# Which queue stores the kept input differences of a two-layer encoder, and when the first input of the down product is split

## The chip, the cores and the metric

The kernel runs on one core of one Trainium2 chip. The core has a matrix engine (TensorE, PE in the profile), a vector engine (VectorE, DVE), an activation engine (ScalarE, ACT), a general engine (GpSimd, POOL) and SyncE (SP), which here only issues DMAs. Each engine works through its own queue in order; ACT, POOL and SP can put DMAs into theirs. The metric is the device time of one execution in microseconds, lower is better.

## The reference

Two encoder layers over 256 tokens of width 2048. Each has an attention sub-layer and an MLP with squared ReLU of width 8192; the change touches the MLP.

```python
for i in range(DEPTH):                      # DEPTH = 2
    h = rms_norm(x, norm_attn[i])
    ...                                     # token mixer and memory attention, one input projection
    x = x + heads @ w_out[i]
    h = rms_norm(x, norm_mlp[i])
    x = x + jnp.square(jax.nn.relu(h @ w_up[i])) @ w_down[i]
```

## The kernel before

**Numbers.** Every float32 operand of a product is split into a high part and a low part (`split`, L441 to L443: ACT casts to the high part, DVE subtracts it for the low part), and a product is three matmuls: high by high, high by low, low by high (`three`, L533 to L536). Weights come from memory as pieces of 128 x 1024 and are split on the chip (`fetch`, L369), two pieces ahead of the one in use (`AHEAD`).

**The MLP** (`mlp`, L997) has two products. `up` makes the 8192 hidden columns in eight steps q of 1024 columns; each step has eight pairs j of inputs. `down` runs over 32 pairs j of hidden inputs, twice, once for each half of the output columns (`half_`).

**Seven instead of eight.** For some pairs (`UP_FAST`, `FAST`, `LATE`) the block product of a pair takes seven block multiplications in place of eight (`seven`, L551). It needs sums of weight blocks (`sum_pair`, L347: four quads, a high and a low part of each of two sums) and differences of input blocks (`differences`, L541: three DVE operations, then a split). For `down`, some of the weight sums are made ahead of time in device memory by POOL's queue (`make_sums`, L285): a copy of one block (L291), and one step later, when the copy has landed, a DMA that adds another block to it (L295). These run during the projections, `out` and `up`; in layer 1 they come closer together during `up` than in layer 0 (`SUM_GAP`: 7 pieces apart, 11 in layer 0).

**Kept differences.** The input differences of `down` are computed while `up` runs, soon after a hidden block exists, and are stored in device memory; both halves of `down` read them back (`load_kept`, L1119 to L1122, POOL's queue, two pairs ahead). There are 17 in each layer (`FAST`), 512 KB each. `keep` (L1008) takes a quad of the tag `h2`, computes the differences into it, and issues the store from POOL's queue (L1013). `to_hidden` (L1023), which transposes a step's result, applies ReLU and square, and may store the hidden block too (L1037, POOL), hands `keep` to the scheduler of small work as one stage.

**Small work.** A `Task` is a list of stages. `tick` (L209) is called twice after every pair; it counts a clock, and runs the stages that are due. A `Light` stage runs at its tick whatever else does; its gap is the number of ticks until the next stage of its task is due.

**Buffers.** `quad` (L91) gives tiles of 4 KB a partition; the tag `h2` has six. During `up` they hold the four parts of a pair's weight sums, the differences of one input pair of `up` (`diffs[2]`, until pair 2 of q = 7), and a kept difference on its way out. During `down` they hold the split inputs (`h2_of`, L1083) and the kept differences read back. The Tile framework gives a tile its place and inserts the waits: whoever writes a place first waits until its last reader, a DMA too, is done. It also settles the order of each engine's queue, near the program's order.

**The boundary of up and down.** After the last pair of q = 7, `own_add` (L1018, four DVE operations, L1021) adds the shared sums to the step's result, and the transposes of `to_hidden` (L1031) read that. Then `down` begins: `load_kept(1)`, the split of input 0 (`ats = deque([h2_of(0)])`, L1125), and from then on the split of input j + 1 while pair j is worked on (L1131). The same lines begin the second half.

Of the kernel before, what the change touches and what calls it, by code (L numbers as in the profile page):

```python
# [15 lines left out]
F32R = mybir.dt.float32r  # L16
# [6 lines left out]
P = 128  # L23
# [30 lines left out]
LOOK = 3  # L54
KEEP_AFTER = (2, 6, 10, 14)
KEEP_LAST = (10, 18, 26, 34)
SUM_AT = {0: 44, 1: 2}
SUM_GAP = ({"in": 4, "mem": 4, "out": 4, "up": 11}, {"in": 4, "mem": 12, "out": 12, "up": 7})
LAM_INIT = 0.8 - 0.6 * math.exp(-0.3 * 0)
# [11 lines left out]
def trunk(ctx: ExitStack, tc: tile.TileContext, xin, xtok, memin, memtok, posrel, gcol, rows,  # L71
# [12 lines left out]
    def nm(s):  # L84
        uid[0] += 1
        return f"{s}{uid[0]}"
# [4 lines left out]
    def quad(tag, shape=(P, 2, 2, 256), dt=F32R):  # L91
        return xp.tile(list(shape), dt, tag=tag, name=nm(tag), bufs={"x2": 8, "h2": 6, "blk": 10}[tag])
# [83 lines left out]
    def Light(f, gap):  # L176
        return Stage(f, gap, gap, True)
# [819 lines left out]
    def mlp(layer, X2, last):  # L997
# [7 lines left out]
        def hidden(j):  # L1005
            return hT[j // 2].rearrange("p k s -> p (k s)")[:, (j % 2) * 512:(j % 2) * 512 + 512]

        def keep(j):  # L1008

            t2 = quad("h2", (P, 2, 512))  # L1010
            differences(t2, hidden(j))
            kept[j] = dp.tile([P, 2, 512], F32R, name=nm("kept"))
            nc.gpsimd.dma_start(kept[j], t2)  # L1013

        name = f"up{layer}"
        diffs = {}
# [6 lines left out]
        def to_hidden(q, n, u, i, tag):  # L1023
            c = 2 * q + n
            if i == 0:
                hT.append(wide[:, 5] if c == 15 else blk([P, 4, S], F32))
            pt = bank(tag)
            for oo in range(2):
                for t in range(2):
                    o = 2 * i + oo  # L1030
                    nc.tensor.transpose(out=pt[:, oo * S + t * P:oo * S + (t + 1) * P], in_=u[n][t][:, o * P:(o + 1) * P], identity=ident)  # L1031
            j = 2 * c + i
            nc.scalar.activation(hidden(j), pt, AF.Relu)
            nc.scalar.activation(hidden(j), hidden(j), AF.Square)
            if c in AWAY:
                hidden_in[j] = dp.tile([P, 512], F32, name=nm("hid"))
                nc.gpsimd.dma_start(hidden_in[j], hidden(j))  # L1037
            if any(j in fast_pairs(f"down{layer}", h) for h in range(2)):
                Task([Light(lambda: keep(j), 0)], wait=KEEP_AFTER[2 * n + i] if q < 7 else KEEP_LAST[2 * n + i])

        for q in range(8):
            tag, other = ("mm", "aux") if q % 2 == 0 else ("aux", "mm")
            own = [[bank(tag) for _ in range(2)] for _ in range(2)]
            fast = UP_FAST[q]
            for j in range(8):
                if j == fast[0]:
                    side = [bank(other) for _ in range(4)]
                if q == 0 and j in DIFF_UP:
                    i = DIFF_UP[j]
                    diffs[i] = quad("h2" if i == 2 else "blk", (P, 2, 512))  # L1050
                    pair_differences(X2.pairs[i], diffs[i])
                two = [piece(name, q, 2 * j + i) for i in range(2)]
                pair = X2.pairs[j]

                def at(kk, t, part):
                    return pair[:, kk, part, t * P:(t + 1) * P]

                if j in fast:
                    seven(own, side, j == fast[0], j == fast[-1], two, sums.pop((name, q, j)), at, diffs[j])
                elif j < 7:  # L1060
                    for kk in range(2):
                        for t in range(2):
                            for n in range(2):
                                one_of_eight(own, n, t, 2 * j + kk, KT - 1, two, at)
                else:
                    for n in range(2):
                        for t in range(2):
                            for kk in range(2):
                                one_of_eight(own, n, t, 2 * j + kk, KT - 1, two, at)
                if j == fast[-1]:  # L1070
                    u = side_sums(side)
                for _ in range(2):
                    tick(2)
            own_add(own, u)
            if q == 0:
                mlp_stats()
            Task([lambda q=q, u=u, n=n, i=i, tag=tag: to_hidden(q, n, u, i, tag) for n in range(2) for i in range(2)], wait=1, gap=0)
        slots.append(blk([P, 4, S], F32))
        N2 = Halves()
        while making:  # L1080
            making.popleft()[1]()

        def h2_of(j):  # L1083
            t2 = quad("h2", (P, 2, 512))
            split(t2[:, 0, :], t2[:, 1, :], hids.pop(j) if j in hidden_in else hidden(j))
            return lambda kk, t, part: t2[:, part, kk * S + t * P:kk * S + (t + 1) * P]

        for half_ in range(2):
            tag = "mm" if half_ == 0 else "aux"
# [32 lines left out]
                    nc.gpsimd.dma_start(diff_in[j], kept[j])  # L1122

            load_kept(1)
            ats = deque([h2_of(0)])  # L1125
            for j in range(32):
                if j == fast[0]:
                    side = [bank("aux" if half_ == 0 else "mm") for _ in range(4)]
                two = [piece(f"down{layer}", half_, 2 * j)]
                if j < 31:  # L1130
                    ats.append(h2_of(j + 1))  # L1131
                load_kept(j + 2)
                two.append(piece(f"down{layer}", half_, 2 * j + 1))
                at = ats.popleft()
# [184 lines left out]
```

## Time and profile before

| | us |
|---|---|
| median of 3 runs | 2078.95 |
| lowest and highest | 2076.1, 2083.54 |
| the profiled execution | 2079.43 |
| its span | 2077.6 |

The times are those of whole executions. The profile is of one execution; its span leaves out 1.8 us around it. An engine's busy time is the time in which it executes instructions; a matrix multiplication's own length overlaps with the next, so two of them start closer together than one is long. Issues of DMAs stand in the queue rows (ACTq, SPq, POOLq, or POOL with a DMA's name) and the time from issue to landing in rows of their own. In the rows of a timeline the brackets hold the idle time of the engine ahead of the instruction and what ended it. The chain of waits goes back from the last instruction, at each step to what released it.

The DMAs that the change touches or that stand in their way, by the profile's list of issues:

| DMA | queue | count | KB | median us to landing |
|---|---|---|---|---|
| kept differences out | POOL | 34 | 512 | 6.8 |
| kept differences in | POOL | 64 | 512 | 5.9 |
| made sums, copy and add | POOL | 124 | 512 | 6.5 |
| hidden blocks out | POOL | 36 | 256 | 4.7 |
| weights of up, plain pairs | SP | 164 | 512 | 5.8 |
| first gains, the only one of ACT | ACT | 1 | 8 | 2.5 |

### The profile page before, as it was taken

Reading aid. Unit: us, or ns where it says so; the run is one execution under the profiler, and the core shown is the slowest. Engines: PE = TensorE matmul, PEld = TensorE weight load, DVE = VectorE, ACT = ScalarE, POOL = GpSimd, SP = SyncE. Lnnn points to the kernel's source line nnn. Section 1 sums busy time; section 2 is a strip of 40 time slices with the busy share of each in tenths; the row PEclk is TensorE's granted clock in tenths of the full one; section 3 lists DMA queues with packets and bytes.
Section 4 is the critical chain, followed back from the end, with each engine's and each line's share of the span. In section 5 each row is a group of like instructions: output and inputs, shape, how many; then the busy total and the mean of one; then the engine's idle time right before and its main releaser. Section 6 shows DMA issues by size and latency. Waiting matters only on the chain.

```text
span 2077.6 us, 28751 instructions
## 1 busy us (share of the span) xinstructions
PE 2068.8 (100%) x9996; PEld 1718.0 (83%) x9996; DVE 1790.4 (86%) x2583; ACT 1280.2 (62%) x1906; POOL 193.2 (9%) x301
## 2 busy tenths in 40 slices
PE   9999999999999999999999999999999999999999
PEld 7888888888888888888888888888888888888887
DVE  7677778898999999998886678889999889999998
ACT  7466665556655676666655556566556567766764
POOL 1201111100010010000001110000101111000000
PEclk9999999999999999999999999999999999999999
DMA  9678988877887789988978987568889998998994
GB/s 312 244 241 276 272 291 232 269 232 218 272 291 259 237 293 329 357 289 282 326 265 273 267 252 228 187 223 244 262 273 293 303 286 309 328 363 309 306 356 168
DMA packets 170641, 572.28 MB, mean 275 GB/s; under 512 B 19744, under 2 KB 20768, under 8 KB 169248
## 3 DMA queue, kind: packets, MB, share of 16 engines
q1 hardware_dynamic: 132976, 440.41, 59.8%
q0 software_dynamic: 37376, 130.04, 23.4%
q8 instruction: 78, 1.28, 0.2%
q14 instruction: 67, 0.55, 0.1%
q10 hardware_dynamic: 144, 0.01, 0.0%
HBM read 537.74 MB, written 97.65 MB: 306 GB/s over the span
## 4 chain that ended last, share of the span: by engine, by line
PE 92%; DMA 2%; DVE 2%; issue 2%; ACT 1%; SPq 0%; POOL 0%; ACTq 0%; DVEq 0%; POOLq 0%
PE mm L535 11%; PE mm L534 11%; PE mm L536 11%; PE aux L535 11%; PE aux L536 11%; PE aux L534 11%; PE mm L495 7%; PE mm L496 7%; PE mm L497 7%; DMA kept<-h 1%; DVE lo L443 1%; PE aux L638 1%; PE mm L1031 1%; PE aux L615 1%; PE aux L657 1%
## 5 line engine op out<-in xcount | busy, mean ns | idle before, releaser
L443 DVE TENSOR_TENSOR lo<-raw,hi 128x1024 fp32r<-128x1024 f32 (+1 forms) x512 | 607.6, 1207 | 168.3 <-ACT hi L442 166.7
L442 ACT CAST hi<-raw 128x1024 fp32r<-128x1024 f32 (+1 forms) x512 | 515.3, 1036 | 377.7 <-PE mm L497 113.9
L495 PE MATMUL mm<-hi,x 128*128 128x512 f32 x640 | 256.7, 403 | 0.7 <-ACT hi L442 0.7
L496 PE MATMUL mm<-lo,x 128*128 128x512 f32 x640 | 250.8, 392 | 0.0
L497 PE MATMUL mm<-hi,x 128*128 128x512 f32 x640 | 250.3, 391 | 0.0
L442 ACT CAST h<-big 128x1024 fp32r<-128x1024 f32 (+1 forms) x100 | 101.1, 1020 | 145.0 <-DVE big L283 90.2
L535 PE MATMUL aux<-lo,h 128*128 128x512 f32 x440 | 171.5, 390 | 0.2 <-DVE lo L443 0.2
L534 PE MATMUL aux<-hi,h 128*128 128x512 f32 x440 | 171.6, 390 | 0.0
L536 PE MATMUL aux<-hi,h 128*128 128x512 f32 x440 | 171.4, 389 | 0.0
L534 PE MATMUL mm<-hi,h 128*128 128x512 f32 (+1 forms) x438 | 170.1, 389 | 0.9 <-ACT h L442 0.9
L535 PE MATMUL mm<-lo,h 128*128 128x512 f32 (+1 forms) x438 | 169.8, 388 | 0.0
L536 PE MATMUL mm<-hi,h 128*128 128x512 f32 (+1 forms) x438 | 169.5, 388 | 0.0
L534 PE MATMUL mm<-hi,x 128*128 128x512 f32 x414 | 161.9, 391 | 0.0
L535 PE MATMUL mm<-lo,x 128*128 128x512 f32 x414 | 161.5, 390 | 0.2 <-DVE lo L443 0.2
L536 PE MATMUL mm<-hi,x 128*128 128x512 f32 x414 | 161.3, 390 | 0.0
L442 ACT CAST hi<-big 128x1024 fp32r<-128x1024 f32 (+1 forms) x146 | 128.9, 911 | 47.8 <-issue 24.5
L535 PE MATMUL aux<-lo,x 128*128 128x512 f32 x398 | 155.3, 390 | 0.5 <-DVE lo L443 0.5
L534 PE MATMUL aux<-hi,x 128*128 128x512 f32 x398 | 155.7, 391 | 0.0
L536 PE MATMUL aux<-hi,x 128*128 128x512 f32 x398 | 155.1, 390 | 0.0
L443 DVE TENSOR_TENSOR lo<-big,hi 128x1024 fp32r<-128x1024 f32 (+1 forms) x146 | 149.1, 1044 | 4.3 <-ACT hi L442 4.3
L497 PEld LDWEIGHTS mm<-hi,x 128*128 128x128 f32 x640 | 120.2, 188 | 26.0
L495 PEld LDWEIGHTS mm<-hi,x 128*128 128x128 f32 x640 | 120.5, 189 | 24.6 <-ACT hi L442 1.1
(310 smaller groups left out, 4268.6 us busy)
## 6 DMA issues: line engine op xcount, KB each, us to landing
raw<-in_w_up SPq DMA_DIRECT2D x164, 512.0 KB, 5.8
raw<-in_w_down SPq DMA_DIRECT2D x128, 512.0 KB, 5.6
madesum<-in_w_down POOLq DMA_DIRECT2D x124, 512.0 KB, 6.5
big<-in_w_up SPq DMA_DIRECT2D x92, 512.0 KB, 4.6
raw<-in_w_a SPq DMA_DIRECT2D x72, 512.0 KB, 4.7
h<-kept POOLq DMA_DIRECT2D x64, 512.0 KB, 5.9
big<-in_w_down SPq DMA_DIRECT2D x54, 512.0 KB, 5.2
big<-madesum SPq DMA_DIRECT2D x53, 512.0 KB, 5.3
```

Source lines behind the costliest of these rows:

```text
L442: nc.scalar.copy(hi, src)
L443: return nc.vector.tensor_tensor(lo, src, as32(hi), op=ALU.subtract)
L495: nc.tensor.matmul(ps[t], lhsT=xh, rhs=hi[:, ws], start=(k == 0), stop=False)
L496: nc.tensor.matmul(ps[t], lhsT=xh, rhs=lo[:, ws], start=False, stop=False)
L497: nc.tensor.matmul(ps[t], lhsT=xl, rhs=hi[:, ws], start=False, stop=(k == KT - 1))
L534: nc.tensor.matmul(acc_, lhsT=x(0), rhs=w2[0][:, ws], start=first_, stop=False)
L535: nc.tensor.matmul(acc_, lhsT=x(0), rhs=w2[1][:, ws], start=False, stop=False)
L536: nc.tensor.matmul(acc_, lhsT=x(1), rhs=w2[0][:, ws], start=False, stop=last_)
L615: nc.tensor.transpose(out=pt[:, h * P:(h + 1) * P], in_=qn[t][:, h * P:(h + 1) * P], identity=ident)
L638: nc.tensor.transpose(out=pt[:, kt * S + qt * P:kt * S + (qt + 1) * P], in_=p_of(qt)[:, kt * P:(kt + 1) * P], identity=ident)
L657: nc.tensor.matmul(ps[c][:, qt * S:(qt + 1) * S], lhsT=qT[a][r, hl, qs], rhs=kT[b][r, hl, :], start=(a + b == 0), stop=(a == 1))
L1031: nc.tensor.transpose(out=pt[:, oo * S + t * P:oo * S + (t + 1) * P], in_=u[n][t][:, o * P:(o + 1) * P], identity=ident)
```

## The change

Two edits, both in the MLP of both layers.

1. `keep` becomes a task of two light stages. `make` takes the quad and computes the differences when `keep` ran before. `store` follows two ticks later (`KEEP_GAP`) and issues the DMA from ACT's queue, source and destination named as plain float32.
2. The split of input 0 of `down` is made ahead of pair 7 of q = 7 in `up`, for the first half, and during pair 31 of the first half, for the second.

```diff
+KEEP_GAP = 2
...
-        def keep(j):
+        def keep(j, wait):
+
+            def make():
+                box.append(quad("h2", (P, 2, 512)))
+                differences(box[0], hidden(j))
+
+            def store():
+                kept[j] = dp.tile([P, 2, 512], F32R, name=nm("kept"))
+                nc.scalar.dma_start(as32(kept[j]), as32(box.pop()))
+
+            box = []
+            Task([Light(make, KEEP_GAP), Light(store, 0)], wait=wait)
 
+        def h2_of(j):
             t2 = quad("h2", (P, 2, 512))
-            differences(t2, hidden(j))
-            kept[j] = dp.tile([P, 2, 512], F32R, name=nm("kept"))
-            nc.gpsimd.dma_start(kept[j], t2)
+            split(t2[:, 0, :], t2[:, 1, :], hids.pop(j) if j in hidden_in else hidden(j))
+            return lambda kk, t, part: t2[:, part, kk * S + t * P:kk * S + (t + 1) * P]
...
-                Task([Light(lambda: keep(j), 0)], wait=KEEP_AFTER[2 * n + i] if q < 7 else KEEP_LAST[2 * n + i])
+                keep(j, KEEP_AFTER[2 * n + i] if q < 7 else KEEP_LAST[2 * n + i])
...
+                if q == j == 7:
+                    ats = deque([h2_of(0)])
                 two = [piece(name, q, 2 * j + i) for i in range(2)]
...
-        def h2_of(j):
-            t2 = quad("h2", (P, 2, 512))
-            split(t2[:, 0, :], t2[:, 1, :], hids.pop(j) if j in hidden_in else hidden(j))
-            return lambda kk, t, part: t2[:, part, kk * S + t * P:kk * S + (t + 1) * P]
-
...
             load_kept(1)
-            ats = deque([h2_of(0)])
             for j in range(32):
...
-                if j < 31:
-                    ats.append(h2_of(j + 1))
+                if j < 31 or half_ == 0:
+                    ats.append(h2_of((j + 1) % 32))
                 load_kept(j + 2)
```

## The prediction, made before the change was run

> **What bounds the kernel now.** I read the page's busy times first, then the time from one group of transposes to the next in both layers, then the chain of waits where that time is longer.
>
> ```profile
> span 2077.6 us, 28751 instructions
> PE 2068.8 (100%) x9996; PEld 1718.0 (83%) x9996; DVE 1790.4 (86%) x2583; ACT 1280.2 (62%) x1906; POOL 193.2 (9%) x301
> ```
>
> TensorE (PE) is busy for all but 9 us. Nothing that shortens another engine's work can gain more than the stalls that PE has left, so the first question is how many there are and who causes them. The up product repeats one period of work per step of q, with 16 transposes (L1031) in each. The chain of waits gives their instants, and the table of windows the two layers' six periods:
>
> ```profile
> 465.11 1.75 PE mm L1031 x16
> ...
> 724.58 1.75 PE mm L1031 x16
> ...
> 1487.42 1.75 PE aux L1031 x16
> ...
> 1575.80 1.75 PE aux L1031 x16
> ...
> 1619.04 1.75 PE mm L1031 x16
> ...
> 1708.56 1.75 PE mm L1031 x16
> ...
> 465.11:724.58 259.47, 259.47 (x1196) 216.38 (x1195) 239.71 (x288) 157.44 (x201) 22.57 (x36) 1.00 0.79 256
> ...
> 1444.18:1708.56 264.38, 261.86 (x1196) 215.83 (x1195) 237.09 (x286) 156.28 (x199) 35.52 (x52) 1.00 0.88 281
> ```
>
> The columns are length, busy time with instruction count of PE, weight loads, DVE, ACT and POOL, granted clock, DMA share, GB/s. Both windows hold 1196 matmuls. Layer 0 does them in 259.47 us, or 43.245 a period, with PE busy throughout; layer 1 takes 264.38. So layer 1 loses **4.91 us** here, at the same granted clock of 1.00. Two of its periods (1487.42 to 1575.80) take 88.38 instead of 86.49, a loss of 1.89; two more (1619.04 to 1708.56) take 89.52, a loss of 3.03. The chain of waits in the first stretch:
>
> ```profile
> 1547.01 1.08 POOL madesum L295
> ...
> 1548.91 11.84 DMA kept<-h
> 1560.85 1.06 ACT h L442
> 1561.93 1.24 DVE h L443
> ...
> 1563.21 0.50 PE mm L535
> ```
>
> This is read downwards. GpSimd issues the accumulating DMA of a made sum (L295), then the store of kept differences (L1013). The store lands 11.84 us later, and only then does ScalarE's cast into a quad begin, then VectorE's low part, then PE. Kept quads and the sums of the up product share six h2 quads: one for the first differences, four for a pair's sums, one for a kept input. A quad is free only when its store has landed. The timelines of ACT, DVE, POOL and PE show the three stalls:
>
> ```profile
> 1546.67 0.61 ACT L442 CAST h<-t2k 128x512 fp32r<-128x512 f32 x1
> 1547.47 2.00 ACT L442 CAST hi<-raw 128x1024 fp32r<-128x1024 f32 x2 [0.20 <-ACT h L442]
> ...
> 1560.85 1.05 ACT L442 CAST h<-big 128x1024 fp32r<-128x1024 f32 x1 [5.92 <-DMA kept<-h]
> ...
> 1640.07 0.62 ACT L442 CAST h<-t2k 128x512 fp32r<-128x512 f32 x1 [2.07 <-DMA kept<-h]
> ...
> 1680.26 2.00 ACT L442 CAST hi<-raw 128x1024 fp32r<-128x1024 f32 x2 [0.20 <-ACT h L442]
> ...
> 1693.04 1.05 ACT L442 CAST h<-big 128x1024 fp32r<-128x1024 f32 x1 [5.32 <-DMA kept<-h]
> ...
> 1547.94 0.68 DVE L443 TENSOR_TENSOR h<-t2k,h 128x512 fp32r<-128x512 f32 x1
> ...
> 1680.72 0.68 DVE L443 TENSOR_TENSOR h<-t2k,h 128x512 fp32r<-128x512 f32 x1
> ...
> 1631.88 0.56 POOL L1013 DMA_DIRECT2D kept<-h  x1
> ...
> 1642.96 0.50 PE L535 MATMUL aux<-lo,x 128*128 128x512 f32 x1 [0.53 <-DVE lo L443]
> ...
> 1695.41 0.50 PE L535 MATMUL aux<-h,blk 128*128 128x512 f32 x1 [0.71 <-DVE h L443]
> ...
> 1698.28 0.50 PE L535 MATMUL mm<-lo,x 128*128 128x512 f32 x1 [0.16 <-DVE lo L443]
> ```
>
> All three waits of ACT end with a store's landing. PE's idle times divide the 3.03 us of the later stretch as 0.53 to 0.87: 1.1 us for the second stall, 1.9 for the third. With 1.9 for the first, that is the whole 4.91.
>
> The other stall is where up ends and down begins, again in PE's and ACT's timelines:
>
> ```profile
> 762.23 1.93 PE L1031 MATMUL aux<-ident,t2k 128*128 128x128 f32 x16
> 764.83 0.50 PE L534 MATMUL mm<-hi,h 128*128 128x512 f32 x1 [0.67 <-ACT h L442]
> ...
> 763.64 0.61 ACT L442 CAST h<-t2k 128x512 fp32r<-128x512 f32 x1
> 764.17 1.13 ACT L442 CAST h<-blk 128x512 fp32r<-128x512 f32 x2
> ...
> 1746.35 1.14 PE L1031 MATMUL aux<-ident,t2k 128*128 128x128 f32 x9
> 1747.79 0.98 PE L1031 MATMUL aux<-ident,t2k 128*128 128x128 f32 x7 [0.29 <-DVE t2k L1021]
> 1748.95 0.50 PE L534 MATMUL mm<-hi,h 128*128 128x512 f32 x1 [0.19 <-ACT h L442]
> ...
> 956.50 0.50 PE L535 MATMUL aux<-lo,h 128*128 128x512 f32 x1 [0.18 <-DVE lo L443]
> ```
>
> Sixteen transposes at their pace of 1.75 us end at 763.98 in layer 0 and would end at 1748.10 in layer 1; the first matmul of down starts 0.85 us after that in each. In layer 0 the cast of down's first input (h<-blk) comes last. In layer 1 own_add on DVE (L1021) holds the transposes, and the cast holds the rest. The last row is PE's wait near the middle of layer 0's down, the one other place that the first input's move could touch.
>
> **The change, part by part.**
>
> *The stores.* 34 stores leave POOL and go to ACT's queue, each issued two ticks (one pair of inputs) after its differences. The rows on which their landing rests, from the kept tile in layer 1's window and in layer 0's, and from the issues of 1545 to 1562:
>
> ```profile
> DMA to landing us min/median/max: 6.2/9.0/11.8
> ...
> DMA to landing us min/median/max: 5.1/6.0/8.0
> ...
> raw<-in_w_up SPq DMA_DIRECT2D x2, 512.0 KB, 9.7
> ```
>
> No store on ACT's queue stands in this trace, so I bound its landing: 6.0 us from below (the store's median in layer 0, with few made sums on POOL) and 9.7 from above (weights of the same size from SP's queue, in the very stretch of the first stall). The issue moves too. In the first stall the low part is done at 1547.94 + 0.68 = 1548.6 and ACT has two casts behind the make, to 1549.5; the store goes out there instead of at 1548.91. It lands at 1555.5 to 1559.2. The landing now is 1560.85 and has to come 1.9 earlier, by 1558.95: 1.65 to 1.9 recovered. In the third, ACT's two casts end at 1682.3, so it lands at 1688.3 to 1692.0, against 1693.0 less 1.9: 1.0 to 1.9 recovered. In the second, issue stays about 1631.9 and the landing is 1637.9 to 1641.6, against 1640.0: all 1.1 recovered, or 1.1 more lost. Together 1.5 to 4.9. I take **4.0**, nearer the lower landing, because the store that was late had an accumulating DMA ahead of it in its own queue and will not have that on ACT's.
>
> The Trainium skill's "DMA: Bandwidth & Descriptors", section "Issuing engines are not separate DMA queues", speaks against this: all engines' DMAs run on the same 16 DMA engines and another issuer saves only issue time. By that rule alone the sum would lose its 4.0, since POOL issued the first late store 0.3 us after its data was ready. The same page, section "SWDGE vs HWDGE vs iDMA", says that the two kinds of queue feed different internal queues between which an engine turns in rotation; by that the 4.0 stands. No run here has yet shown a store on ACT's queue.
>
> *What the stores cost ACT.* The one DMA that ACT issues today, and what waiting does to an issuing queue:
>
> ```profile
> 0.74 0.41 ACTq L129 DMA_DIRECT2D gc<-in_gcol  x1
> ...
> SPq L387 <- DVE lo L443: 804.1, 403, 12.6
> ```
>
> 34 issues at 0.41 are 14 us of ACT, 17 a layer. In the up windows ACT is busy 157 of 259 us and its idle time is spent waiting for PE and DVE, which covers 13 x 0.41 = 5.3 us a window. The second row is the danger: a queue whose DMA waits for DVE stands still with all that is behind it, here the casts of the next weight pieces, for which DVE's low parts and then PE wait. The delay from the make's cast to the end of its low part is 1548.6 - 1546.67 = 1.95 us, and the two casts between make and store take 2.0, so the wait is mostly over when the store's turn comes. The bounds: nothing, or a standstill long enough to reach PE. The second stall measures that: 2.07 us of ACT's waiting cost 1.1 of PE, so about 1.0 us is free. I take 0. A later release of the quad can also delay the next make's cast by up to a pair's time; the same spare applies.
>
> *POOL* loses 34 issues of 0.56 us and has its made sums and reads alone. It bounds nothing, so I give that nothing.
>
> *The first input of down, a pair sooner.* Its cast (0.61) and low part (about 0.65) move ahead of pair 7 of q = 7. Nothing is added but the earlier use of an h2 quad, which is there, since pair 6's sums are read by then. In layer 0 PE can go on at once: up to 0.85 gained. If the transposes still run first, the 0.65 us on DVE ahead of own_add gives some 0.25 back: 0.6. I take 0.7. In layer 1 own_add is what the transposes wait for. If the first matmuls of down go ahead of the transposes, 0.85 is gained; if not, own_add ends 0.65 later and 0.25 is lost. I take 0.5. At the middle of down (half 0 to half 1) I give nothing: PE's idle time there is 0.18, and it ends with the low part of a weight piece, not of the input.
>
> *Sum:* 4.0 + 0.7 + 0.5 = 5.2 off the profiled execution's 2079.43, so 2074.2. That execution stands 0.5 above the median of the three runs, 2078.95; I forecast **2074.0**, between the two bases.
>
> **The rivals.**
>
> *All of it goes:* 4.9 + 0.85 + 0.85 = 6.6 off, and a few tenths more if other short waits fall with them: 2072.3. For it speaks that layer 0, with the same up product, has no stall at all; against it that DMA is at 0.88 in layer 1's window and 0.79 in layer 0's.
>
> *The landing is set by the traffic.* With the 9.7 us of SP's own loads in that stretch as the rule and the store issued up to a pair later, no net time is won in up: only the 1.2 at the boundaries stays, 2078.2. For it: the loads on SP's queue were as slow as the stores. The Trainium skill's section on issuing engines, named above, would have it so. Against it: those two loads shared SP's queue with others, while the store has ACT's to itself.
>
> *Slower: ACT's queue stands still at the stores.* Where DVE lags by more than about 1.0 us behind the store's place on ACT, or the next kept cast waits for a store issued a pair later, the casts of weights come late. The point from which it decides is that 1.0 us. Priced at what layer 1 loses today, layer 0's six periods lose 4.9 and layer 1's a second 4.9, less 1.2 at the boundaries: +8.6, 2088.0. Against it: the 1.95 us lag above, and ACT's being idle for 39% of the window.
>
> **How the numbers follow.** Forecast 0.50 (own range 2072 to 2077), all of it 0.20, traffic 0.20, slower 0.10. The range 2071 to 2081 leaves out the slower case, most of which lies above, and the far end of the full gain. 0.3%, which is 6.2 us, is about what a measurement of this kernel can tell from no change. Faster by more: 0.15 from the full gain, 0.05 from the forecast's better end, 0.20. Slower by more: 0.09, the last case less a part that costs less. The rest, 0.71, is within.
>
> **What would show it.** Right: layer 1's six up periods take 259.5 to 261 us; stores land in 6 to 8 us beside an accumulating DMA; ACT no longer waits 5 us for a kept landing; the transposes of the last q stand behind down's first matmuls, or without idle time ahead of them. Wrong: layer 0's 259.47 grows; DMA issues on ACT wait for DVE by more than 1 us; stores land in 9 us or more with the same stalls; the idle time before down's first matmul stays.

## The result, and the profile after

| | before | after |
|---|---|---|
| median of 9 runs, us | 2078.95 | 2072.9 |
| lowest and highest, us | 2076.1, 2083.54 | 2071.96, 2073.38 |
| the profiled execution, us | 2079.43 | 2072.64 |
| its span, us | 2077.6 | 2070.9 |

The ratio of the times is 0.9967, with a 95% interval of 0.9958 to 0.9977. That is 0.33% faster, or 6.05 us between the medians. The interval has the line of 0.3% inside it, so a change of more than 0.3% and one of less can barely be told apart here.

The profile after, first its page: the busy times, and the shares of the chain of waits by engine.

```profile
PE 2065.5 (100%) x9996; PEld 1718.5 (83%) x9996; DVE 1784.3 (86%) x2583; ACT 1278.6 (62%) x1906; POOL 173.7 (8%) x267
PE 99%; DMA 0%; DVE 0%; issue 0%; ACT 0%; SPq 0%; ACTq 0%; DVEq 0%
```

The same line of the chain before:

```profile
PE 92%; DMA 2%; DVE 2%; issue 2%; ACT 1%; SPq 0%; POOL 0%; ACTq 0%; DVEq 0%; POOLq 0%
```

The matmuls are the same 9996. What went is the 7% of the chain that passed through DMAs, casts, subtractions and issues. That is a share of the chain and not time won: PE was busy beside most of it. The windows show where time was won. First after, the six periods of up in layer 0 and in layer 1 (columns as in the prediction), then the 100 us that begin with the transposes of q = 6, for each layer:

```profile
464.68:724.16 259.48, 259.48 (x1197) 216.32 (x1195) 236.09 (x287) 156.36 (x200) 15.40 (x23) 1.00 0.78 256
1443.11:1702.59 259.48, 259.48 (x1196) 216.32 (x1195) 236.29 (x287) 156.63 (x200) 27.98 (x39) 1.00 0.89 286
...
724.16:824.16 100.00, 100.00 (x460) 83.33 (x458) 94.07 (x116) 71.43 (x95) 7.49 (x14) 1.00 0.88 308
...
1702.59:1802.59 100.00, 100.00 (x459) 83.33 (x458) 94.80 (x117) 72.22 (x96) 7.55 (x14) 1.00 0.92 317
```

The same 100 us before:

```profile
724.58:824.58 100.00, 99.33 (x455) 82.57 (x453) 94.05 (x116) 70.64 (x94) 9.64 (x18) 1.00 0.87 302
...
1708.56:1808.56 100.00, 99.52 (x455) 82.24 (x453) 94.51 (x118) 71.74 (x95) 9.68 (x18) 1.00 0.92 315
```

The six up periods of layer 1 fell from 264.38 to 259.48, the time of layer 0, at a DMA share that is no lower (0.89). All 4.90 us are back. In the 100 us around the end of up, PE starts 5 matmuls more in layer 0 and 4 more in layer 1. At 0.22 to 0.23 us from one start to the next (761.58 to 761.80 below) these 9 are about **2.0 us**, good to one matmul in each layer. Together that is 6.9; the spans differ by 6.7. The account isn't exact to a few tenths: the transposes that begin layer 0's window come 0.43 earlier (464.68 against 465.11), though neither edit touches what is ahead of them.

**The stores.** ACT's timeline where the first stall was, after:

```profile
1545.54 0.62 ACT L443 CAST h<-t2k 128x512 fp32r<-128x512 f32 x1
1546.41 2.00 ACT L443 CAST hi<-raw 128x1024 fp32r<-128x1024 f32 x2 [0.25 <-ACT h L443]
1547.53 0.33 ACTq L1017 DMA_DIRECT2D kept<-h  x1
```

Two things are to be seen. The store (L1017) goes out between the two casts of one group, not behind them. And it comes 17.93 us into its period (which begins at 1529.60), against 18.24 before (1548.91, in the period that began 43.25 after 1487.42). The list of DMA issues of that instant, after and then before, gives KB and the time to landing:

```profile
kept<-h ACTq DMA_DIRECT2D x1, 512.0 KB, 8.3
```

```profile
kept<-h POOLq DMA_DIRECT2D x1, 512.0 KB, 11.8
```

So here 3.5 of the 3.8 us by which the landing is earlier come from a shorter flight, and 0.3 from an earlier issue. The second stall went in another way. DVE's timeline before, with the low part that the store waits for, and DVE's and ACT's after:

```profile
1630.90 0.68 DVE L443 TENSOR_TENSOR h<-t2k,h 128x512 fp32r<-128x512 f32 x1
```

```profile
1625.43 0.68 DVE L444 TENSOR_TENSOR h<-t2k,h 128x512 fp32r<-128x512 f32 x1
...
1626.15 0.33 ACTq L1017 DMA_DIRECT2D kept<-h  x1
```

Before, the low part ends at 1631.58 and the store goes out at 1631.88, 12.84 us into its period; after, the low part ends at 1626.11 and the store goes out 0.04 us later, 10.05 into its period. So POOL's order didn't hold the store. Of the 2.8 us, 2.5 are that the differences themselves are made earlier, in another order of ACT's and DVE's work, and 0.3 is the issue. Two other runs with the store on ACT's queue, stores only and one stage, have the same 10.05; the runs with POOL's or SP's have 11.8 to 12.8. The flight is no shorter (8.8 after, 8.1 before). In the third stall the flight falls from 11.2 to 9.3 us, and the issue comes 0.3 earlier in its period. All 13 stores of layer 1's window (1443 to 1703) together, by the kept tile, after:

```profile
  DVE h L444: 1.9, 1
  ACT h L443: 0.4, 1
...
DMA to landing us min/median/max: 5.0/8.4/9.3
```

The first two rows are who waited for a store (us in all, times). Before, ACT waited 14.0 us in four times, and landings were 6.2/9.0/11.8. DVE's 1.9 now costs PE nothing, by the windows.

**The end of up**, PE's timeline in layer 0, and then in layer 1:

```profile
761.58 0.39 PE L537 MATMUL aux<-hi,x 128*128 128x512 f32 x1
761.80 0.39 PE L535 MATMUL mm<-hi,h 128*128 128x512 f32 x1
...
767.25 1.91 PE L1043 MATMUL aux<-ident,t2k 128*128 128x128 f32 x16
...
1740.00 0.39 PE L537 MATMUL aux<-hi,x 128*128 128x512 f32 x1
1740.23 0.39 PE L535 MATMUL mm<-hi,h 128*128 128x512 f32 x1
```

The last matmul of up (aux) is followed by the first of down (mm) at the usual distance, in both layers. The transposes (L1043) stand 5.45 us later, behind down's first pair, and nothing waits for own_add. Near the middle of layer 0's down, in PE's timeline after:

```profile
954.33 0.50 PE L536 MATMUL aux<-lo,h 128*128 128x512 f32 x1 [0.23 <-DVE lo L444]
955.46 0.50 PE L536 MATMUL aux<-lo,h 128*128 128x512 f32 x1 [0.17 <-DVE lo L444]
```

Two waits, 0.40 us, where before there was one of 0.18. That the sooner split causes the second isn't shown: with it and the stores on SP's queue there is one, of 0.17.

### The profile page after: what moved, and what is told of

It is laid out like the page before. It is cut to its first block, busy times and chain, and to the rows that moved or that the text cites. A ratio compares the mean times of both kernels' runs of the same rounds, so it can differ in the third digit from the quotient of the medians.

```text
span 2070.9 us, 28741 instructions
## 1 busy us (share of the span) xinstructions
PE 2065.5 (100%) x9996; PEld 1718.5 (83%) x9996; DVE 1784.3 (86%) x2583; ACT 1278.6 (62%) x1906; POOL 173.7 (8%) x267
## 4 chain that ended last, share of the span: by engine, by line
PE 99%; DMA 0%; DVE 0%; issue 0%; ACT 0%; SPq 0%; ACTq 0%; DVEq 0%
PE mm L537 12%; PE mm L536 12%; PE mm L535 12%; PE aux L536 12%; PE aux L537 12%; PE aux L535 12%; PE mm L496 7%; PE mm L497 7%; PE mm L498 7%; PE aux L639 1%; PE aux L1043 1%; PE mm L1043 1%; PE aux L616 1%; PE aux L658 1%; PE aux L696 1%; PE aux L845 0%
## 5 line engine op out<-in xcount | busy, mean ns | idle before, releaser
L498 PEld LDWEIGHTS mm<-hi,x 128*128 128x128 f32 x640 | 120.3, 188 | 26.1
L444 DVE TENSOR_TENSOR h<-big,h 128x1024 fp32r<-128x1024 f32 (+1 forms) x100 | 116.5, 1179 | 28.5 <-ACT h L443 25.7
```

The source lines that it names most:

```text
L444: return nc.vector.tensor_tensor(lo, src, as32(hi), op=ALU.subtract)
L498: nc.tensor.matmul(ps[t], lhsT=xl, rhs=hi[:, ws], start=False, stop=(k == KT - 1))
```

## The experiments

The ratios are to the kernel before, with their 95% intervals. "Up" is the length of the six up periods of layer 1, found from the transposes' starts; it is 264.38 before and 259.48 after. L1017 is the store in the kernel after.

| run | median us | ratio | up, layer 1 |
|---|---|---|---|
| stores only | 2076.75 | 0.9990 [0.9981, 0.9999] | 259.48 |
| sooner split only | 2078.34 | 0.9996 [0.9987, 1.0005] | 263.79 |
| after, stores on POOL | 2075.87 | 0.9987 [0.9978, 0.9996] | 262.73 |
| after, stores on SP | 2072.88 | 0.9972 [0.9962, 0.9982] | 259.72 |
| after, one stage | 2072.94 | 0.9975 [0.9965, 0.9985] | 259.48 |
| before, no adding DMA | 2073.19 | 0.9973 [0.9963, 0.9983] | 259.47 |
| before, store reads elsewhere | 2073.76 | 0.9978 [0.9968, 0.9988] | 259.48 |
| the same, at the old times | 2074.39 | 0.9978 [0.9969, 0.9988] | 259.85 |
| after, each store in halves | 2073.62 | 0.9973 [0.9963, 0.9983] | 259.47 |
| after, stores a pair later | 2075.03 | 0.9983 [0.9974, 0.9992] | 259.83 |
| after, ACT held at the stores | 2093.47 | 1.0073 [1.0058, 1.0088] | 266.16 |
| after, POOL, stores late | 2095.16 | 1.0079 [1.0064, 1.0094] | 269.92 |

### Each edit alone

Stores on ACT's queue, the split of input 0 where it was:

```diff
-                if q == j == 7:
-                    ats = deque([h2_of(0)])
...
             load_kept(1)
+            ats = deque([h2_of(0)])
...
-                if j < 31 or half_ == 0:
-                    ats.append(h2_of((j + 1) % 32))
+                if j < 31:
+                    ats.append(h2_of(j + 1))
```

> Stores on ACT's queue two ticks after the make, down's first input split where it was. Theory (the two edits are independent, the stores are worth 4.9 us in layer 1's up, the sooner split 0.85 at each end of up): layer 1's six up periods 259.5 us, the idle time of 0.2 to 0.7 us ahead of down's first matmul back in both layers, about 1.7 us above the changed kernel, ratio to before 0.9975. Rival (the stores alone disturb the order, the sooner split hides it): periods over 260 us, ratio above 0.998.

The sooner split, the stores as before:

```diff
+            def whole():
+                t2 = quad("h2", (P, 2, 512))
+                differences(t2, hidden(j))
                 kept[j] = dp.tile([P, 2, 512], F32R, name=nm("kept"))
-                nc.scalar.dma_start(as32(kept[j]), as32(box.pop()))
+                nc.gpsimd.dma_start(kept[j], t2)
...
-            Task([Light(make, KEEP_GAP), Light(store, 0)], wait=wait)
+            Task([Light(whole, 0)], wait=wait)
```

> Stores on GpSimd's queue in one stage as before, down's first input split a pair sooner. Theory: layer 1's six up periods stay at 264.4 us with stores that land 11 us after their issue, down's first matmul follows up's last at once in both layers; 1.7 us below before, ratio 0.9992. Rival (the sooner split changes the order in up too and takes part of the 4.9): periods under 263 us, ratio under 0.998.

Measured: 2076.75 and 2078.34. Their windows, stores only (the ends of both layers, and layer 1's up), then PE's timeline at the end of up in layer 0:

```profile
724.00:824.00 100.00, 99.12 (x452) 81.99 (x451) 93.08 (x115) 70.24 (x93) 7.50 (x14) 1.00 0.89 302
1445.08:1704.56 259.48, 259.48 (x1196) 216.32 (x1195) 236.45 (x288) 156.54 (x200) 28.03 (x39) 1.00 0.90 287
1704.56:1804.56 100.00, 99.12 (x452) 81.99 (x451) 93.07 (x115) 69.95 (x93) 7.56 (x14) 1.00 0.90 308
```

```profile
762.47 1.13 PE L1043 MATMUL aux<-ident,t2k 128*128 128x128 f32 x8 [0.42 <-DVE t2k L1033]
...
764.39 0.50 PE L535 MATMUL mm<-hi,h 128*128 128x512 f32 x1 [0.19 <-ACT h L443]
```

And with the sooner split only:

```profile
1442.85:1706.64 263.79, 261.81 (x1196) 215.78 (x1195) 237.10 (x287) 156.18 (x199) 35.48 (x52) 1.00 0.89 282
1706.64:1806.64 100.00, 100.00 (x459) 83.15 (x457) 95.78 (x119) 72.49 (x95) 9.87 (x19) 1.00 0.93 314
```

Each edit does its own part: the stores remove the stall in up, the split removes the one at the end. They are not simply added, and the expected 0.9975 for the stores alone was missed (0.9990). With the stores alone PE starts 452 matmuls at each end, 3 fewer than before, about 0.7 us: own_add now keeps the transposes waiting in layer 0 too. So the stores alone bring 4.9 - 1.4 = 3.5 us by these windows (the spans say 2.9), and the sooner split is worth more beside them (the spans of stores only and of after differ by 3.8) than by itself. Alone, its profiled execution is 2.8 shorter, but that was one of the faster ones of a wide spread: the medians differ by less than 1, and the interval of its ratio has 1 inside. DVE comes to own_add later with the stores moved because its order is another: before, the low parts of four weight pieces are done by 757.4 and own_add begins at 759.26; with the stores alone two of them start at 756.54 and 758.87, and own_add begins at 760.93.

### The queue, apart from the second stage

The kernel after with its stores on POOL's queue, the two stages kept:

```diff
-                nc.scalar.dma_start(as32(kept[j]), as32(box.pop()))
+                nc.gpsimd.dma_start(as32(kept[j]), as32(box.pop()))
```

> As the changed kernel (two stages, two ticks apart, sooner split), but the store goes out on GpSimd's queue. Theory (a queue of its own is what counts): the stores still stand behind the made sums' DMAs, layer 1's six up periods 264 us or more, ratio 0.9990 to 1.000. Rival (the two stages and the order that follows from them are what counts, the queue is not): periods 259.5 us, ratio 0.9967. Second rival (what counts is that GpSimd's accumulating DMAs no longer wait behind the stores): periods as in the theory, and made sums that land later.

The same line with SyncE's queue (`nc.sync`):

> As the changed kernel, but the store goes out on SP's queue among the loads of weights. Theory (a store must not stand behind GpSimd's made sums, in their queue of transfers or in GpSimd's order; any other queue will do): layer 1's six up periods at most 261 us, stores land in 8 us or less, ratio 0.997 to 0.998. Rival (it has to be a queue without other traffic): SP stands at the stores until VectorE has their low part, weights come late, periods 262 us or more in layer 1 and over 259.5 in layer 0 as well.

ACT's queue, make and store in one stage:

```diff
-            Task([Light(make, KEEP_GAP), Light(store, 0)], wait=wait)
+            Task([Light(lambda: (make(), store()), 0)], wait=wait)
```

> As the changed kernel, but the store is issued in the same stage as its differences, on ACT's queue, so ACT's queue may wait there for VectorE's low part (1.95 us from the make's cast to the end of its low part in the profile before). Theory (1.0 us of standstill of ACT is free, one of 2 us costs about 1): ACT stands 1 to 2 us at a store in up, at the 34 stores together up to 10 us lost where it reaches PE, ratio 0.998 to 1.001. Rival (the framework's order puts other casts between make and store in any case, or ACT's spare covers it): periods 259.5 us in both layers, ratio 0.9967, KEEP_GAP without effect.

On POOL, the window of layer 1's up, its kept tile, and the chain of waits ahead of a loss in the second period and at the third stall:

```profile
1443.55:1706.28 262.73, 261.46 (x1195) 215.76 (x1194) 236.99 (x287) 156.31 (x199) 35.47 (x52) 1.00 0.88 283
...
  ACT h L443: 11.8, 4
...
DMA to landing us min/median/max: 6.0/9.5/11.4
...
1476.57 10.27 DMA raw<-in_w_up
...
1677.82 1.10 POOL madesum L296
...
1679.46 11.37 DMA kept<-h
```

On SP, the same window and landing:

```profile
1442.44:1702.16 259.72, 259.72 (x1195) 216.34 (x1194) 238.07 (x287) 156.65 (x199) 27.98 (x39) 1.00 0.88 286
...
DMA to landing us min/median/max: 4.7/7.8/10.7
```

With every other line as in the kernel after, the queue alone is worth 262.73 - 259.48 = 3.25 us in up and 2.97 in the medians. The store is named as plain float32 here too, so the naming isn't what did it. In the sixth period, of 45.22, the old picture is back: the adding DMA, the store right behind it, a landing 11.4 us later, 2.0 us lost. Another 1.0 is lost in the second period, of 44.23, and there the chain goes back to a piece of weights that took 10.27 us on SP's queue, not to a store. The other 1.7 of the 4.9 isn't assigned by these runs. The second rival finds no support: the made sums of this window land at a median of 7.2 us with the stores on POOL and 6.9 in the kernel after. That the new queue is ACT's doesn't matter to the time: SP's does as well. But the expected landings in 8 us or less were missed there, with 10.7 at the longest. One stage instead of two gives 2072.94 and 259.48, the kernel after within what a measurement can tell; the framework puts other casts between most makes and their stores of its own accord, so `KEEP_GAP` isn't what did it.

### The adding DMA

The kernel before, where the adding DMA of each made sum is replaced by a read of 32 bytes a partition on the same queue, so that the sums aren't formed:

```diff
-            nc.gpsimd.dma_start(made_in[name, h, j], upper.unsqueeze(1).broadcast_to([P, 2, 512]), accum_op=ALU.add)
+            nc.gpsimd.dma_start(little, made_in[name, h, j][:, 0, 0:8])
```

> The kernel before, with each made sum's adding DMA (512 KB) replaced by one that waits for the same copy and moves 32 bytes a partition; the sums of weights in down are then not formed. GpSimd waits as before, but no large adding transfer stands ahead of the stores. Theory A (the transfer ahead of the store in its own queue makes it land late): stores land in 6 to 8 us, the first and third stall go, layer 1's six up periods 259.5 to 261 us. Theory B (GpSimd's waiting for the copy before it gets to the store is what makes it late): periods 263 us or more, landings short. Whole time 2 to 7 us under before, since the ends of up keep their 1.7.

The window, and the landing of the stores, which are on POOL as before:

```profile
1442.76:1702.23 259.47, 259.47 (x1195) 216.41 (x1194) 239.52 (x289) 157.35 (x201) 27.60 (x52) 1.00 0.77 262
...
DMA to landing us min/median/max: 5.2/6.2/7.4
```

The stall is gone without the change. But the DMA share fell too, from 0.88 to 0.77, so by itself this doesn't separate the queue's order from the traffic. For the stall the runs above do: on ACT's or SP's queue the share is 0.88 to 0.89 and the stall is gone all the same. The landings are less clear-cut. These are the stores of layer 1's window that go out at most 3 us behind an adding DMA, from the timelines of POOL and of the store's queue:

| run | store's queue | to landing, us | median |
|---|---|---|---|
| before | POOL | 8.4 to 11.8 | 9.7 |
| after, stores on POOL | POOL | 7.8 to 11.4 | 10.7 |
| after | ACT | 7.7 to 9.3 | 8.4 |
| after, stores on SP | SP | 6.5 to 10.7 | 8.5 |

Without the adding DMA the median of all 13 is 6.2. So another queue takes 1.2 to 2.3 us off such a landing, and some 2 us of what the adding DMA costs stay on ACT's and SP's too. The packets that moved show it, in the kernel after. Its store went out on ACT's queue (q10) at 1547.53; these are the adding DMA's (q0) in 1549 to 1551.5, as packets, MB and share of the 16 DMA engines, when no packet of q10 moved, and then the store's in 1551.5 to 1556:

```profile
q0 software_dynamic: 171, 0.35, 100.0%
...
q10 hardware_dynamic: 144, 0.52, 28.5%
```

### The quad that the store holds

The kernel before, where the stores of j under 28 read a tile of the normed input and not the quad, which is then free as soon as its differences are made; down reads other values back:

```diff
+            if j < 28:
+                t2 = X2.pairs[0].rearrange("p k a s -> p k (a s)")
             nc.gpsimd.dma_start(kept[j], t2)
```

> The kernel before, but the stores of hidden inputs 0 to 27 read the split inputs of up's pair 0 instead of the kept differences, so the same bytes go through the same queue behind the same adding DMAs and no store holds an h2 quad; down then reads wrong differences back. Theory (the only way from the store to PE is the quad that it holds): layer 1's six up periods 259.5 us with stores that still land in 9 to 11 us; ends of up as before; about 5 us under before, ratio 0.9976. Rival (the queue of made sums and stores delays PE in another way, by the loads of weights): periods 263 us or more.

2073.76, but it doesn't answer the question: with nothing to wait for, stores went out early (from 381 us on, the last of them at 1385.5, ahead of layer 1's up), so the traffic moved too. The DMA share of layer 1's up window fell to 0.84. The next run makes each store wait for its low part, as before:

```diff
-            differences(t2, hidden(j))
+            low = differences(t2, hidden(j))
...
-            nc.gpsimd.dma_start(kept[j], t2)
+            ins = nc.gpsimd.dma_start(kept[j], t2)
+            tc.add_manual_dep(ins.ins, low.ins.name, mybir.DependencyInfo(mybir.DependencyClass.Sync, mybir.DependencyReason.DATA),
+                              reason="behind the low part")
```

> As e11_other_source (stores of inputs 0 to 27 read up's pair 0, so no store holds an h2 quad; down reads wrong differences back), with each store made to wait for the low part of its differences, so that it goes out where it did before, behind the adding DMAs in GpSimd's queue; in e11 the stores had gone out early. Theory (the only way from a late store to PE is the quad that it holds): several stores of layer 1 land 9 to 11 us after their issue, as before, and yet the six up periods take 259.5 us; ratio 0.9976. Rival (the queue of made sums and stores delays PE in another way, say by the loads of weights): periods 263 us or more.

```profile
1443.00:1702.48 259.48, 259.44 (x1194) 215.88 (x1193) 239.98 (x288) 156.89 (x200) 35.65 (x52) 1.00 0.91 289
...
DMA to landing us min/median/max: 6.4/8.9/11.6
...
1546.98 1.08 POOL L295 DMA_DIRECT2D madesum<-in_w_down  x1 [6.00 <-DMA madesum<-in_w_down]
1548.97 0.56 POOL L1015 DMA_DIRECT2D kept<-x  x1 [0.90 <-DVE h L443]
```

This is a window of the same length, the kept tile and POOL's timeline. The stores leave at the old instants (1548.97, against 1548.91), behind the same adding DMA, and land as late as before, with more traffic (0.91). Yet PE is busy for all but 0.04 us of the window, and from transposes to transposes up takes 259.85. The 0.37 us over 259.48 are lost in the second period, where the chain goes back to a piece of weights that took 9.70 us, as on POOL above. So when no quad hangs on them, late landings cost 0.4 us at most in place of 4.9: the quad is by far the main way by which they reach PE. A seventh quad, the plain form of this test, wasn't tried.

### What the stores cost ACT, and what lateness costs

Twice the issues, each store as two halves on ACT's queue:

```diff
-                nc.scalar.dma_start(as32(kept[j]), as32(box.pop()))
+                t2 = box.pop()
+                for i in range(2):
+                    nc.scalar.dma_start(as32(kept[j])[:, i], as32(t2)[:, i])
```

> As the changed kernel, each store issued as two of half the size, one behind the other: 68 issues on ACT's queue in place of 34. Theory (34 issues of 0.33 us, 11 us together, lie in ACT's idle time): no change within the measurement, six up periods 259.5 us in both layers. Rival (an issue costs the path): 4 to 11 us more.

2073.62, up at 259.47: 68 issues for 34 show no cost in up, and the 0.7 us between the medians is about the spread of either kernel.

The stores a pair later, each held behind the newest cast:

```diff
-KEEP_GAP = 2
+KEEP_GAP = 4
...
-                nc.scalar.dma_start(as32(kept[j]), as32(box.pop()))
+                with tc.issue_after(newest[0].ins):
+                    nc.scalar.dma_start(as32(kept[j]), as32(box.pop()))
```

> As the changed kernel, but the store is held back to four ticks after its make and behind the casts that stand before it in the program: one pair, some 4 to 5 us, later on ACT's queue. Theory (what counts is when the store has landed, and in the changed kernel VectorE still waits 1.9 us for one landing without loss to PE, so about 1 to 2 us are left): the stalls are back, ACT or VectorE wait for landings by some 3 us a time, layer 1's six up periods 262 us or more and layer 0's over 259.5, ratio 0.998 or above. Rival (the landing is not what set the time; the free queue on GpSimd or the new order is): periods 259.5 us in both layers, ratio 0.997.

The store that left at 1547.53 in the kernel after leaves at 1556.59, in a trace that runs 1.7 us later. That is 7.4 us later in its period, and up takes 259.83, where the expectation had 262 or more. That expectation failed. Leaving later cost 0.35 us in up. Part of the reason is that this store no longer has an adding DMA close ahead of it and lands in 5.4 us in place of 8.3, so it lands 4.5 later and not 7.4. Another, which wasn't tested: the later issue is known when the program is built, and the quads are given out around it. The median is 2.1 above the kernel after, most of it outside up.

Make and store in one stage, and no later cast may pass the store on ACT:

```diff
     def split(hi, lo, src):
-        nc.scalar.copy(hi, src)
+        if gate:
+            with tc.issue_after(gate[0]):
+                nc.scalar.copy(hi, src)
+        else:
+            nc.scalar.copy(hi, src)
...
+                gate.append(nc.scalar.dma_start(as32(kept[j]), as32(t2)).ins)
```

> As the changed kernel, but every store stands on ACT's queue right behind its make's cast (at most one other instruction between) and no later cast of a weight piece may pass it: ACT's queue waits at each of the 34 stores until VectorE has written the low part, about 1 to 2 us. This is the slower rival of the prediction, made to happen. By the price put there (1.0 us of standstill is free, what is over reaches PE): 26 stores in the up windows, up to 1 us each, 5 to 15 us slower than the changed kernel, six periods over 260 us in both layers. If ACT's idle time covers it: 259.5 us in both, no change.

The windows of both layers, and ACT's timeline at one store:

```profile
464.34:730.54 266.20, 262.51 (x1195) 215.22 (x1194) 235.39 (x288) 156.80 (x200) 15.39 (x23) 1.00 0.78 250
1453.72:1719.88 266.16, 262.47 (x1195) 215.24 (x1194) 235.31 (x288) 157.02 (x200) 28.17 (x39) 1.00 0.89 279
...
1559.48 0.62 ACT L447 CAST h<-t2k 128x512 fp32r<-128x512 f32 x1
1561.47 0.33 ACTq L1021 DMA_DIRECT2D kept<-h  x1
1561.84 2.00 ACT L447 CAST hi<-raw 128x1024 fp32r<-128x1024 f32 x2 [1.74 <-PE mm L542]
```

ACT's cast ends at 1560.10, and its next begins at 1561.84: 1.74 us in which the queue stands at a DMA that waits for DVE's low part (the row names PE as the releaser; the store in between shows what it was). There are thirteen such stands in a window, of 0.5 to 2.0 us. Together they cost 266.2 - 259.48 = 6.7 us of PE, 0.5 each on average, in layer 0 too, where there was never a stall. They don't all cost the same: of the six periods one loses nothing and one 3.2 us. The whole execution is 20.6 us above the kernel after; 13.4 of that is in the two windows, and where the rest goes wasn't followed.

POOL's queue, `KEEP_GAP` 4, and each store waiting for the newest cast:

```diff
-                nc.scalar.dma_start(as32(kept[j]), as32(box.pop()))
+                ins = nc.gpsimd.dma_start(as32(kept[j]), as32(box.pop()))
+                tc.add_manual_dep(ins.ins, newest[0].ins.name, mybir.DependencyInfo(mybir.DependencyClass.Sync, mybir.DependencyReason.DATA),
+                                  reason="behind a cast")
```

> GpSimd's queue again, two stages and sooner split as in the changed kernel, but the store waits until ACT has made the cast that is newest four ticks after the make: one to two pairs later than in the kernel before, and known to the framework when it gives out the quads. Theory P (a late store costs only where the framework has planned a quad on an earlier landing; told of the late issue it plans around it): layer 1's six up periods 259.5 to 260.5 us although the stores land later in the period than before. Theory Q (the queue itself is what counts): the stores again stand behind the adding DMAs, periods 262 us or more.

2095.16, up at 269.92 in layer 1 and 262.61 in layer 0. One period alone takes 53.69, and ACT's longest wait for a store is 11.1 us. Some 4 of the 10.4 us lost in that period are the clock: after PE had idled 5.48 us, its granted clock was 0.50 from 1656 to 1664.6, and matmuls started 0.43 us apart. The run mixes two things, stores that leave late and a POOL queue that stands with the made sums behind it, and can't say how much each is worth, so it decides nothing between the two theories: late stores on ACT's queue were nearly harmless, late stores together with a standing POOL queue were not.

## Why the prediction was right, and where it was not

**The bound** was read rightly: the stalls of layer 1's up periods and those at the ends of up were all that these edits could reach, and they are what went.

**The stores: the mechanism was right, the size too small.** The step "I take 4.0" failed as a size: 4.90 came. The landing was bounded as 6.0 to 9.7, and the three stores that stalled came at 8.3, 8.8 and 9.3: inside, but near the far end, where the prediction had leaned to the near one. What it got wrong besides is the issue. It put each store behind two casts, 0.6 later than POOL's in the first and third stall, and left the second's where it was. In fact the store slips in between the two casts, 0.3 us earlier in the period than POOL's, and in the second stall, where the prediction counted a loss of 1.1 as one end of its bounds, it goes out 2.8 earlier. With the flights that came and the issues as forecast, its own working gives 1.9 - 0.7 + 1.4 = 2.6. So that 4.0 was near is in part luck: the flights were longer than it took, and the issues earlier, above all because the differences of the second store came to be made 2.5 us sooner, which nothing in the prediction foresaw. The reason for leaning to the lower landing, that the adding DMA would no longer stand ahead in the store's own queue, is borne out in kind and weaker than it was told: the median falls from 9.7 to 8.4 us, and to 6.2 only where the adding DMA is taken out.

This bears on the two sections of the Trainium skill's "DMA: Bandwidth & Descriptors" that the prediction weighed. By "Issuing engines are not separate DMA queues", moving the issue should save issue time only. The first stall's flight, 3.5 us shorter where the issue came 0.3 earlier, is more than that. "SWDGE vs HWDGE vs iDMA", with separate internal queues taken in turn, agrees with 262.73 against 259.48 for the same kernel on two queues. But the turns weren't even here: the first store's packets came only after most of the adding DMA's, as shown above.

**The ends of up: right in kind, low in size.** "I take 0.7" and "I take 0.5" are 1.2; the windows show about 2.0. The favourable branch of both cases held (the first matmuls of down go ahead of the transposes, in both layers), and I had hedged it against the other. The full 0.85 for each would have been 1.7, as near as the count of matmuls can tell.

**The middle of down** was given nothing, and PE's idle time there grew by 0.2, which isn't shown to be the edit's. **POOL** was given nothing, rightly; **ACT's issues** at 0, rightly, as the halves show.

**The rivals.** "All of it goes", 2072.3 at a chance of 0.20, is the case that came: all three stalls and both ends are gone (2072.9, which the forecast's own range of 2072 to 2077 holds too). "The landing is set by the traffic" is refuted as it was priced: the share stayed at 0.89 and the stall went. Something of it is true all the same, as the landings of 8.4 us beside an adding DMA show, and the forecast's sign of 6 to 8 us was missed. The slower rival, "ACT's queue stands still", didn't happen. The prediction had about 1.0 us of standstill free, taken from one stall, and priced the case at 2088.0. Held on purpose, stands of 0.5 to 2.0 us cost 0.5 each on average in both layers and the run took 2093.47: the rival was dearer than it was priced. Two things keep the change from it. One is the cast between make and store on which the prediction counted, though it is one and not two. In ACT's and DVE's timelines of the kernel after, at the third stall's place:

```profile
1676.15 2.00 ACT L443 CAST hi<-raw 128x1024 fp32r<-128x1024 f32 x2 [0.24 <-ACT h L443]
1677.28 0.33 ACTq L1017 DMA_DIRECT2D kept<-h  x1
...
1676.56 0.68 DVE L444 TENSOR_TENSOR h<-t2k,h 128x512 fp32r<-128x512 f32 x1
```

The low part ends at 1677.24, while ACT is casting; the store goes out 0.04 us later, and ACT doesn't stand. The other is that where no cast stands between, the work behind the store isn't ready either. ACT's timeline 20 us earlier, where the make's cast ends at 1655.77:

```profile
1657.31 0.33 ACTq L1017 DMA_DIRECT2D kept<-h  x1
1658.69 1.57 ACT L443 CAST hi<-big 128x1024 fp32r<-128x1024 f32 x2 [2.92 <-PE mm L537]
```

Here the queue does stand at the store for 1.5 us, which the prediction had named as a sign of being wrong. It costs nothing, because the next cast waits for PE until 1658.69 anyway.

## What to carry to other kernels

When a buffer's release hangs on a store, look at when the store's data is ready and at what lies ahead of it in its own DMA queue, and not at the traffic alone: here another queue, ACT's or SP's, took 3 us off at the same traffic, though it made the landings only 1 to 2 us shorter. A DMA put on a working engine's queue costs next to nothing when its data is ready as its turn comes, or when the work behind it isn't ready either. Where it held ready work back, it cost half a microsecond of the bound engine each time on average, so see that something stands between the maker and the store. Two edits that meet at one place should be priced together: here the stores alone gave back part of what they won at a boundary that the second edit then removed.

## What was not expected of the hardware

A 512 KB store at most 3 us behind an adding DMA of the same size took 8.4 to 11.8 us to land on POOL's queue in the kernel before; with that DMA gone the longest was 7.4. On ACT's queue beside it it took 7.7 to 9.3: moving the store to another queue doesn't get it out of the adding DMA's way altogether.

The runs of the kernel before lie 7.4 us apart (2076.1 to 2083.54), those after 1.4. The sooner split alone, where ACT still waits for stores, has 7.4 as well (2074.86 to 2082.25), while stores on SP (2.1), one stage (1.4), halves (1.9) and no adding DMA (2.4) are narrow. It may be that late landings differ from run to run. But stores only, without such waits, has one run at 2080.32 and lies 5.2 apart, and the kernel after with its stores on POOL, which has them, only 4.1, so it isn't settled.
